# Two plain gate and up steps at the head of each half step of a decoder block, with the residual reloaded by another queue

## The chip, the core and the metric

The kernel runs on one core of one Trainium2 chip. A core has TensorE (matrix products into PSUM, here called PE), VectorE (DVE), ScalarE (ACT), GpSimd (POOL) and SyncE (SP, which here only issues transfers). Each works through its own list of instructions in order, and waits on semaphores where it needs another's result. The metric is the device time of one execution in microseconds.

## The reference: what is computed

```python
x = x + 0.5 * swiglu(rms_norm(x, ffn1_norm), w_gate1, w_up1, w_down1)     # first half step
h = rms_norm(x, mix_norm); z = h @ w_in                                   # mixing: gMLP and attention
x = x + m(z) @ w_out
x = x + 0.5 * swiglu(rms_norm(x, ffn2_norm), w_gate2, w_up2, w_down2)     # second half step

def swiglu(h, w_gate, w_up, w_down):
    return (jax.nn.silu(h @ w_gate) * (h @ w_up)) @ w_down
```

There are 512 tokens, a width of 1024 and 2816 hidden columns in each half step; everything is float32.

## The kernel before

Activations lie with the features on the partitions: eight tiles `x` of 128 features by 512 tokens. Every product is made of three matmuls of rounded parts (`w_hi`·`x_hi`, `w_hi`·`x_lo`, `w_lo`·`x_hi`); a helper, `split` (lines 139 and 140), makes the parts of a weight tile: a cast on ACT to `hi`, a subtraction on DVE to `lo`. The norm's gain is applied when `xg_hi` and `xg_lo` are made (`normed_input`, lines 180 and 181); the norm's scale `r_bc` is multiplied in behind the products. `norm_scale` makes it: two matmuls with ones sum the squares (`sq_hi` and `sq_lo`, lines 194 and 195), ACT takes the root, DVE makes one Newton step (lines 158 to 160).

**A half step** is the function `ffn`. It goes through 22 blocks of 128 hidden columns, two at a time; such a pair is a `q` ("quad"), so there are eleven. After quads 0 to 3 a **down group** adds their part of the result (line 377 loads the down weights, eight output tiles `j`, 24 matmuls of 512 columns each), after quads 4 to 7 another, after 8 to 10 a last one (18 matmuls for each `j`). In the last group line 387 adds the part, line 389 multiplies by `r_bc`, and `finish` adds the residual: it reloads `x` into a `scratch` tile by a transfer that POOL issues (line 482; line 949 in the second half step), and line 483 (950) adds it. In the first half step `finish1` then makes `xg` and the squares of the next norm, and writes `y` to `x1_dram` through POOL; in the second, SP writes the output.

A quad in its ordinary form, `quad`, takes seven half-size products in place of eight (four blocks of gate and up, combined by sums of weights, line 307, and sums of activations): 168 matmuls of 256 columns, line 320. The first product takes `xg` as it is (A11), the second takes the sums `s_hi`, `s_lo` of `half_sums`. `add_sums` makes those once for a half step, on DVE, for four pairs of tiles `kt` and `kt + 4`: two products with the gain (line 218), four sums (lines 221 to 224) and a `split`. The first half step starts with a **plain** quad instead, `first_quad`: 96 matmuls of 512 columns (lines 125 to 127), in an order that needs only `xg`, with weights in quarters of a tile while `x` still comes in; `add_sums` follows it. The second half step starts with `add_sums` and an ordinary quad 0.

Weights pass through `w_raw` tiles (two shared, four of the half step's own pool) and `w_hi`, `w_lo` tiles (three shared, one own). The own tiles of the second half step lie where the mixing's tiles lay, and can be written only after its last matmul. A scheduler lays the instructions of each engine in a fixed order at build time; a transfer that waits holds up the SP queue behind it.

Between the half steps, `pump` runs the mixing's weight units. The first four are `w_qk`, 24 matmuls each (lines 529 to 531), in the order: two units, the norm's two matmuls of `norm_scale`, a third unit, four transposes of `r_bc` (line 899), the fourth. At its end, eight units of `add_out` (line 869) make the tiles `x` of the second half step one after the other.

## Time and profile before

| | us |
|---|---|
| median of 3 runs (1195.34 to 1196.57) | 1195.42 |
| the profiled execution | 1197.43 |
| its span, from the first to the last instruction | 1195.6 |
| PE busy | 1156.7 (97%) |
| DVE busy | 868.6 (73%) |
| ACT busy | 600.5 (50%) |

Times below are microseconds from the start of the span. In the table of stretches a row holds the stretch, its length, the busy time and (in brackets) the instructions of PE, of PE's weight loads, of DVE, ACT and POOL, then the granted clock of PE (1.00 is 2.4 GHz, 0.50 is 1.2 GHz), the DMA engines' busy share and their GB/s. In a row of the timeline the numbers are start and duration; "[4.90 <-ACT sq_hi L139]" says that the engine stood idle 4.90 us before it and what ended that; "x5" that five such rows are merged. Durations of neighbours overlap a little, so a pace is read from start to start. A matmul's duration is its latency, longer than its pace.

### The profile page before, as it was taken

The page shows a single profiled execution, that of the slowest core. Times are in us where ns is not written, and L with a number is a line of the kernel's source. Part 1 is how long each engine was busy: PE and PEld are TensorE (multiplying, and loading weights), DVE is VectorE, ACT ScalarE, POOL GpSimd, SP SyncE. Part 2 cuts the span into 40 slices and gives each one's busy share as a digit, 9 for nine tenths or more (in the row PEclk, how much of TensorE's full clock was granted, in tenths as well). Part 3 has the DMA queues.
Part 4 walks back from the last instruction along what each step waited for, and adds up shares of the span by engine and source line. Part 5 has one row for each costly group of instructions (what it writes and reads, how often), then busy time and mean ns, then how long its engine had stood idle before and what let it go on. Part 6 is the DMA issues. An engine that isn't in the chain of part 4 may idle for free.

```text
span 1195.6 us, 17191 instructions
## 1 busy us (share of the span) xinstructions
PE 1156.7 (97%) x6834; PEld 1017.2 (85%) x6834; DVE 868.6 (73%) x1342; ACT 600.5 (50%) x869; POOL 37.1 (3%) x74
## 2 busy tenths in 40 slices
PE   9699999999998999999999999999699999999998
PEld 7699899989986888888888778887699889988996
DVE  7996379747877667876778876555998459855875
ACT  7454256414544454557687966333475335532540
POOL 0000000000002000000000001000000000000000
PEclk9799999999999999999999999999799999999999
DMA  7134133422335332231212124333325322441332
GB/s 247 49 101 151 56 109 107 144 68 86 120 104 164 118 89 89 60 99 59 76 62 66 46 83 145 102 115 126 112 75 159 121 66 78 136 128 53 107 124 88
DMA packets 47983, 122.11 MB, mean 102 GB/s; under 512 B 4512, under 2 KB 6592, under 8 KB 47904
## 3 DMA queue, kind: packets, MB, share of 16 engines
q1 hardware_dynamic: 44160, 109.07, 28.8%
q0 software_dynamic: 3744, 11.96, 3.1%
q8 instruction: 53, 0.87, 0.3%
q14 instruction: 26, 0.21, 0.1%
HBM read 114.72 MB, written 6.29 MB: 101 GB/s over the span
## 4 chain that ended last, share of the span: by engine, by line
PE 89%; DVE 4%; ACT 3%; DMA 2%; issue 1%; POOL 0%; POOLq 0%; DVEq 0%; ACTq 0%
PE bank_acc L320 22%; PE bank_att L320 12%; PE bank_acc L125 10%; PE bank_acc L126 9%; PE bank_acc L127 9%; PE bank_acc L530 4%; PE bank_acc L531 4%; PE bank_acc L529 4%; PE bank_att L126 4%; PE bank_att L127 4%; PE bank_att L125 4%; DMA scratch<-in_x 1%; PE bank_att L658 1%; PE bank_att L659 1%; PE bank_att L684 1%
## 5 line engine op out<-in xcount | busy, mean ns | idle before, releaser
L139 ACT CAST w_hi<-w_raw 128x1024 fp32r<-128x1024 f32 (+2 forms) x195 | 189.5, 979 | 273.7 <-PE bank_acc L126 93.2
L140 DVE TENSOR_TENSOR w_lo<-w_raw,w_hi 128x1024 fp32r<-128x1024 f32 (+2 forms) x195 | 220.0, 1133 | 69.5 <-ACT w_hi L139 68.2
L139 ACT CAST w_hi<-w_sum 128x1024 fp32r<-128x1024 f32 x84 | 88.2, 1050 | 146.6 <-PE bank_acc L320 63.1
L320 PE MATMUL bank_acc<-s_hi,w_hi 128*128 128x256 f32 x504 | 142.4, 283 | 0.9 <-ACT w_hi L139 0.9
L320 PE MATMUL bank_acc<-s_lo,w_hi 128*128 128x256 f32 x504 | 142.0, 282 | 0.0
L320 PE MATMUL bank_acc<-s_hi,w_lo 128*128 128x256 f32 x504 | 141.8, 281 | 0.0
L140 DVE TENSOR_TENSOR w_lo<-w_sum,w_hi 128x1024 fp32r<-128x1024 f32 x84 | 102.3, 1219 | 28.5 <-ACT w_hi L139 28.5
L320 PEld LDWEIGHTS bank_acc<-s_hi,w_hi 128*128 128x128 f32 x504 | 95.6, 190 | 1.6 <-ACT w_hi L139 1.5
L320 PEld LDWEIGHTS bank_acc<-s_lo,w_hi 128*128 128x128 f32 x504 | 95.4, 189 | 0.0
L320 PEld LDWEIGHTS bank_acc<-s_hi,w_lo 128*128 128x128 f32 x504 | 95.4, 189 | 0.0
L529 PE MATMUL bank_acc<-w_hi,xg_hi 128*128 128x512 f32 x224 | 90.5, 404 | 0.0
L530 PE MATMUL bank_acc<-w_lo,xg_hi 128*128 128x512 f32 x224 | 89.6, 400 | 0.0
L531 PE MATMUL bank_acc<-w_hi,xg_lo 128*128 128x512 f32 x224 | 89.3, 399 | 0.0
L320 PE MATMUL bank_acc<-xg_lo,w_hi 128*128 128x256 f32 x256 | 72.1, 282 | 0.0
L320 PE MATMUL bank_acc<-xg_hi,w_hi 128*128 128x256 f32 x256 | 72.0, 281 | 0.0
L320 PE MATMUL bank_acc<-xg_hi,w_lo 128*128 128x256 f32 x256 | 72.0, 281 | 0.0
L125 PE MATMUL bank_acc<-xg_hi,w_hi 128*128 128x512 f32 x176 | 70.8, 402 | 1.1 <-ACT w_hi L139 1.1
L320 PE MATMUL bank_att<-s_hi,w_hi 128*128 128x256 f32 x168 | 49.7, 296 | 21.7 <-ACT w_hi L139 21.7
L127 PE MATMUL bank_acc<-xg_hi,w_lo 128*128 128x512 f32 x176 | 70.4, 400 | 0.0
L126 PE MATMUL bank_acc<-xg_lo,w_hi 128*128 128x512 f32 x176 | 70.3, 399 | 0.0
L320 PE MATMUL bank_att<-xg_lo,w_hi 128*128 128x256 f32 x248 | 69.8, 282 | 0.0
L320 PE MATMUL bank_att<-xg_hi,w_hi 128*128 128x256 f32 x248 | 69.7, 281 | 0.0
(271 smaller groups left out, 2944.9 us busy)
## 6 DMA issues: line engine op xcount, KB each, us to landing
w_raw<-in_gu SPq DMA_DIRECT2D x84, 512.0 KB, 3.8
w_raw<-in_dn SPq DMA_DIRECT2D x32, 512.0 KB, 3.6
w_raw<-in_w_qk SPq DMA_DIRECT2D x16, 512.0 KB, 3.7
w_raw<-in_dn SPq DMA_DIRECT2D x16, 384.0 KB, 3.2
w_raw<-in_w_v SPq DMA_DIRECT2D x8, 512.0 KB, 3.6
w_raw<-in_w_ga SPq DMA_DIRECT2D x8, 512.0 KB, 3.5
w_raw<-in_w_gb SPq DMA_DIRECT2D x8, 512.0 KB, 3.6
w_raw<-in_w_pb SPq DMA_DIRECT2D x8, 512.0 KB, 3.6
```

Of the source, the lines that this page charges most:

```text
L125: nc.tensor.matmul(ps, lhsT=lhi, rhs=rhi, start=first, stop=False)
L126: nc.tensor.matmul(ps, lhsT=lhi, rhs=rlo, start=False, stop=False)
L127: nc.tensor.matmul(ps, lhsT=llo, rhs=rhi, start=False, stop=last)
L139: latest["hi"] = nc.scalar.copy(hi, src)
L140: latest["lo"] = nc.vector.tensor_tensor(lo, src, hi, op=ALU.subtract)
L320: nc.tensor.matmul(o, lhsT=l[:, s], rhs=r, start=first and f == kt == i == 0, stop=kt == HK - 1 and i == 2, skip_group_check=True,)
L529: nc.tensor.matmul(banks[t], lhsT=xg_hi[k][:, ts], rhs=hi[:, s], start=k == 0, stop=False)
L530: nc.tensor.matmul(banks[t], lhsT=xg_hi[k][:, ts], rhs=lo[:, s], start=False, stop=False)
L531: nc.tensor.matmul(banks[t], lhsT=xg_lo[k][:, ts], rhs=hi[:, s], start=False, stop=k == KD - 1)
L658: nc.tensor.matmul(s[m], lhsT=qd[m][:, qs], rhs=kd[m][:, :w], start=True, stop=False)
L659: nc.tensor.matmul(s[m], lhsT=ql[m][:, qs], rhs=kd[m][:, :w], start=False, stop=False)
L684: nc.tensor.transpose(ps[:, j * P : (j + 1) * P], a[:, j * P : (j + 1) * P], ident)
```

## The change

Quads 0 and 1 of both half steps are plain (`plain_quad`), and `add_sums` comes after quad 1. `add_sums` no longer multiplies whole tiles by the gain: ACT makes one scaled half tile, and four DVE instructions take `x` directly, with the gain or its negative (`neg_gains`, new) as a factor; the sums lie in tiles that the results of quads 2 and 3 take later. The second column block of the first quad loads and splits each weight tile whole, no longer in quarters. The residual is reloaded as four `x_again` tiles, through SP, in the program ahead of the last down group, into the tiles of the weight sums (`w_sum`) and of `g`; the addition stands in `ffn`. `add_out` runs in the order 0, 4, 1, 5, 2, 6, 3, 7.

```diff
         def add(kt, x1, x2):
-            y = []
-            for j, xt in ((kt, x1), (kt + HK, x2)):
-                y.append(scratch())
-                g = gains[:, norm * KD + j : norm * KD + j + 1]
-                nc.vector.tensor_scalar(y[-1], xt, g, None, op0=ALU.mult)
-            f = pool.tile([P, 4, HT], F32, name="sums", tag="g", bufs=2)
-            (a11, a21), (a12, a22) = ((t[:, :HT], t[:, HT:]) for t in y)
-            nc.vector.tensor_tensor(f[:, 1], a11, a21, op=ALU.subtract)
-            nc.vector.tensor_tensor(f[:, 0], a22, a21, op=ALU.subtract)
...
+            (x11, x21), (x12, x22) = ((t[:, :HT], t[:, HT:]) for t in (x1, x2))
+            f = pool.tile([P, 4, HT], F32, name="sums", tag=("a_hi", "a_lo")[kt % 2] + str(2 + kt // 2))
+            a21 = scratch()[:, :HT]
+            nc.scalar.activation(a21, x21, AF.Copy, scale=g1)
+            add = partial(nc.vector.scalar_tensor_tensor, op0=ALU.mult, op1=ALU.subtract)
+            add(f[:, 1], x11, g1, a21)
+            add(f[:, 0], x22, g2, a21)
+            add(f[:, 2], x22, neg, f[:, 1])
+            add(f[:, 3], x12, neg, f[:, 2])
...
-        def first_quad():
+        def plain_quad(q):
...
+                loading = load is not None and q == f == 0
+                cuts = 4 if loading else 1
...
-                    if k % 2 == 0:
-                        cs = slice(k * P, (k + 2) * P)
+                    if k % (KD // cuts) == 0:
+                        cs = slice(k * P, k * P + D // cuts)
                         for e in range(2):
-                            nc.sync.dma_start(out=raws[e][:, cs], in_=gu[f, e, :, cs])
+                            nc.sync.dma_start(out=raws[e][:, cs], in_=gu[2 * q + f, e, :, cs])
                             split(w[e][0][:, cs], w[e][1][:, cs], raws[e][:, cs])
...
-                if q == 0 and load is not None:
-                    first_quad()
+                if q < 2:
+                    plain_quad(q)
+                else:
+                    quad(q)
+                if q == 1:
                     for kt in range(HK):
                         add_sums(kt, xt[kt], xt[kt + HK])
-                    continue
-                if q == 0:
-                    for kt in range(HK):
-                        add_sums(kt, xt[kt], xt[kt + HK])
-                quad(q)
+            if f0 + n == NF:
+                for i in range(HK):
+                    tag = ("w_sum", "g")[i // 2]
+                    back.append(pool.tile([P, 2, T], F32, name="x_again", tag=tag, bufs=2))
+                    again(back[i], i)
...
                     nc.vector.tensor_tensor(y[j], y[j], r_bc, op=ALU.mult)
+                    nc.vector.scalar_tensor_tensor(
+                        y[j], y[j], -0.5, back[j // 2][:, j % 2], op0=ALU.mult, op1=ALU.add
+                    )
                     finish(j, y[j])
...
         def finish1(j, y):
-            xr = scratch()
-            nc.gpsimd.dma_start(out=xr, in_=x[:, j, :])
-            nc.vector.scalar_tensor_tensor(y, y, -0.5, xr, op0=ALU.mult, op1=ALU.add)
...
+        def again1(t, i):
+            nc.sync.dma_start(out=t, in_=x[:, 2 * i : 2 * i + 2, :])
...
-        for n in range(KD):
+        for n in (n for kt in range(HK) for n in (kt, kt + HK)):
             add_out(n)
```

**VectorE in the first plain quad**, while it sums the squares of `x` (`sq_sum`) and splits the weights of the second column block. Before:

```order
L189 TENSOR_TENSOR sq_sum_119<-sq_sum_119,scratch_277 128x512
L140 TENSOR_TENSOR w_lo_301<-w_raw_304,w_hi_300 128x256
L189 TENSOR_TENSOR sq_sum_119<-sq_sum_119,scratch_280 128x512
L140 TENSOR_TENSOR w_lo_303<-w_raw_305,w_hi_302 128x256
L189 TENSOR_TENSOR sq_sum_119<-sq_sum_119,scratch_283 128x512
L140 TENSOR_TENSOR w_lo_301<-w_raw_304,w_hi_300 128x256
L140 TENSOR_TENSOR w_lo_303<-w_raw_305,w_hi_302 128x256
```

Now:

```order
L190 TENSOR_TENSOR sq_sum_120<-sq_sum_120,scratch_279 128x512
L190 TENSOR_TENSOR sq_sum_120<-sq_sum_120,scratch_282 128x512
L140 TENSOR_TENSOR w_lo_303<-w_raw_306,w_hi_302 128x1024
L190 TENSOR_TENSOR sq_sum_120<-sq_sum_120,scratch_285 128x512
L140 TENSOR_TENSOR w_lo_305<-w_raw_307,w_hi_304 128x1024
L140 TENSOR_TENSOR w_lo_376<-w_raw_379,w_hi_375 128x1024
L140 TENSOR_TENSOR sq_lo_290<-sq_sum_120,sq_hi_289 128x512
```

The first split of that block stands one sum later and covers a whole tile, and the splits of quad 1 (`w_lo_376` is the first) follow at once.

**The SP queue around the last down group of the first half step** (`in_gu1`: gate and up weights, `in_dn1`: down weights, `in_w_qk`: the mixing's). Before:

```order
L303 DMA w_raw_3117<-in_gu1 128x2x512
L377 DMA w_raw_3350<-in_dn1 128x768
L377 DMA w_raw_3384<-in_dn1 128x768
L377 DMA w_raw_3420<-in_dn1 128x768
L377 DMA w_raw_3456<-in_dn1 128x768
L377 DMA w_raw_3492<-in_dn1 128x768
L377 DMA w_raw_3528<-in_dn1 128x768
L377 DMA w_raw_3564<-in_dn1 128x768
L377 DMA w_raw_3600<-in_dn1 128x768
L116 DMA w_raw_3640<-in_w_qk 128x1024
```

Now, from the third down load on:

```order
L384 DMA w_raw_3302<-in_dn1 128x768
L497 DMA x_again_3225<-in_x 128x1024
L384 DMA w_raw_3336<-in_dn1 128x768
L497 DMA x_again_3227<-in_x 128x1024
L384 DMA w_raw_3370<-in_dn1 128x768
L384 DMA w_raw_3404<-in_dn1 128x768
L497 DMA x_again_3229<-in_x 128x1024
L384 DMA w_raw_3438<-in_dn1 128x768
L384 DMA w_raw_3472<-in_dn1 128x768
L497 DMA x_again_3231<-in_x 128x1024
L116 DMA w_raw_3510<-in_w_qk 128x1024
```

The four reloads stand behind the third, fourth, sixth and eighth down load.

**VectorE behind the last `add_out`**, at the head of the second half step. Before:

```order
L869 TENSOR_TENSOR x1_7_7238<-x1_7_7238,bank_acc_7800 128x512
L218 TENSOR_SCALAR scratch_7837<-x1_0_7224,gains_79 128x512
L181 SCALAR_TENSOR_TENSOR xg_lo7_116<-x1_7_7238,gains_79,xg_hi7_108 128x512
L189 TENSOR_TENSOR sq_sum_119<-sq_sum_119,scratch_7828 128x512
L218 TENSOR_SCALAR scratch_7839<-x1_4_7232,gains_79 128x512
L221 TENSOR_TENSOR sums_7841<-scratch_7837 128x256
```

Now:

```order
L880 TENSOR_TENSOR x1_7_7108<-x1_7_7108,bank_acc_7670 128x512
L182 SCALAR_TENSOR_TENSOR xg_lo7_117<-x1_7_7108,gains_79,xg_hi7_109 128x512
L190 TENSOR_TENSOR sq_sum_120<-sq_sum_120,scratch_7698 128x512
L140 TENSOR_TENSOR sq_lo_7772<-sq_sum_120,sq_hi_7771 128x512
L140 TENSOR_TENSOR w_lo_7785<-w_raw_7788,w_hi_7784 128x1024
L140 TENSOR_TENSOR w_lo_7787<-w_raw_7789,w_hi_7786 128x1024
```

The squares and the weights of quad 0's second column block (`w_raw_7788`, `w_raw_7789`) come first, and the sums only after the norm.

## Rows read from the trace of the kernel before

**Rows 1.** The page: engine totals, and PE's clock in 40 slices.

```profile
PE 1156.7 (97%) x6834; PEld 1017.2 (85%) x6834; DVE 868.6 (73%) x1342; ACT 600.5 (50%) x869; POOL 37.1 (3%) x74
...
PEclk9799999999999999999999999999799999999999
```

**Rows 2.** Waits of PE over the span: total, times, longest.

```profile
PE bank_att L320 <- ACT w_hi L139: 21.7, 2, 12.0
```

**Rows 3.** Stretches: heads, ordinary quads, a down group, the seam to the mixing.

```profile
31.07:65.54 34.47, 23.59 (x169) 22.80 (x168) 32.16 (x43) 16.66 (x18) 0.00 (x0) 0.80 0.20 62
65.54:105.46 39.92, 39.92 (x338) 39.92 (x337) 35.46 (x36) 22.05 (x25) 0.00 (x0) 1.00 0.42 133
105.46:149.97 44.51, 44.51 (x194) 36.06 (x193) 17.39 (x16) 13.14 (x17) 0.00 (x0) 1.00 0.26 75
378.69:393.08 14.39, 9.49 (x31) 7.15 (x31) 7.09 (x9) 5.55 (x8) 6.31 (x11) 0.76 0.45 143
831.83:928.43 96.60, 83.36 (x675) 82.49 (x674) 89.72 (x106) 53.43 (x60) 0.54 (x1) 0.91 0.39 123
```

**Rows 4.** PE's timeline at the first head, and its first matmuls.

```profile
8.34 0.63 PE L127 MATMUL bank_att<-xg_hi,w_lo 128*128 128x512 f32 x1
8.77 0.63 PE L125 MATMUL bank_acc<-xg_hi,w_hi 128*128 128x512 f32 x1
...
43.73 0.58 PE L320 MATMUL bank_att<-s_hi,w_hi 128*128 128x256 f32 x1 [9.67 <-ACT w_hi L139]
```

**Rows 5.** VectorE's work from 26 to 47 us, by group (count, busy us, mean ns).

```profile
L140 DVE TENSOR_TENSOR s_lo<-sums,s_hi 128x1024 fp32r<-128x1024 f32 x4 | 4.9, 1220 | 0.0
L218 DVE TENSOR_SCALAR scratch<-x,gains 128x512 f32<-128x512 f32 x8 | 3.8, 478 | 0.0
...
L223 DVE SCALAR_TENSOR_TENSOR sums<-sums,scratch 128x256 f32<-128x256 f32 x4 | 1.7, 414 | 0.0
```

**Rows 6.** DVE's timeline in the first plain quad.

```profile
15.10 3.87 DVE L189 TENSOR_TENSOR sq_sum<-sq_sum,scratch 128x512 f32<-128x512 f32 x5
18.89 0.42 DVE L140 TENSOR_TENSOR w_lo<-w_raw,w_hi 128x256 fp32r<-128x256 f32 x1
```

**Rows 7.** Stretches again: 10 to 20 us, in the first plain quad.

```profile
10.00:20.00 10.00, 10.00 (x43) 8.05 (x42) 9.26 (x18) 9.98 (x23) 0.00 (x0) 1.00 0.96 330
```

**Rows 8.** Seam to the mixing: the reload (a line's view), waits, timelines of POOL, DVE and PE.

```profile
DMA to landing us min/median/max: 2.9/3.8/4.5
...
DVE y L483 <- DMA scratch<-in_x: 8.8, 6, 2.3
...
376.29 0.54 POOL L482 DMA_DIRECT2D scratch<-in_x  x1
...
367.49 0.40 PE L529 MATMUL bank_acc<-w_hi,xg_hi 128*128 128x512 f32 x1
383.75 0.79 PE L194 MATMUL bank_att<-sq_hi,ones_r 128*128 128x512 f32 x1 [4.90 <-ACT sq_hi L139]
...
379.95 0.69 DVE L483 SCALAR_TENSOR_TENSOR y<-y,scratch 128x512 f32<-128x512 f32 x1 [2.33 <-DMA scratch<-in_x]
380.56 1.22 DVE L140 TENSOR_TENSOR w_lo<-w_raw,w_hi 128x1024 fp32r<-128x1024 f32 x1
```

**Rows 9.** Last down group of the first half step: SP, DVE (timelines).

```profile
303.87 26.59 SPq L377 DMA_DIRECT2D w_raw<-in_dn  x8
...
318.22 1.22 DVE L140 TENSOR_TENSOR w_lo<-w_sum,w_hi 128x1024 fp32r<-128x1024 f32 x1
...
338.24 1.23 DVE L140 TENSOR_TENSOR a_lo<-g,a_hi 128x1024 fp32r<-128x1024 f32 x1 [1.17 <-ACT a_hi L139]
```

**Rows 10.** Second head: PE and DVE timelines, and a stretch.

```profile
846.86 0.58 PE L320 MATMUL bank_att<-s_hi,w_hi 128*128 128x256 f32 x1 [12.03 <-ACT w_hi L139]
...
826.43 0.69 DVE L869 TENSOR_TENSOR x<-x,bank_acc 128x512 f32<-128x512 f32 x1 [2.22 <-PE bank_acc L127]
...
835.00:840.00 5.00, 0.00 (x0) 0.00 (x0) 5.00 (x13) 1.05 (x1) 0.00 (x0) 0.68 1.00 376
```

More of the change, by code (lines that the diff above doesn't have):

```diff
@@ L145, in decoder_block @@
     eps_col = const.tile([P, 1], F32, name="eps_col")
+    neg_gains = const.tile([P, 3 * KD], F32, name="neg_gains")
     nc.gpsimd.dma_start(out=gains, in_=cols)
@@ L213, in add @@
         def add(kt, x1, x2):
-            y = []
-            for j, xt in ((kt, x1), (kt + HK, x2)):
-                y.append(scratch())
-                g = gains[:, norm * KD + j : norm * KD + j + 1]
-                nc.vector.tensor_scalar(y[-1], xt, g, None, op0=ALU.mult)
-            f = pool.tile([P, 4, HT], F32, name="sums", tag="g", bufs=2)
-            (a11, a21), (a12, a22) = ((t[:, :HT], t[:, HT:]) for t in y)
-            nc.vector.tensor_tensor(f[:, 1], a11, a21, op=ALU.subtract)
-            nc.vector.tensor_tensor(f[:, 0], a22, a21, op=ALU.subtract)
-            nc.vector.scalar_tensor_tensor(f[:, 2], f[:, 0], -1.0, a11, op0=ALU.mult, op1=ALU.subtract)
-            nc.vector.scalar_tensor_tensor(f[:, 3], a12, -1.0, f[:, 2], op0=ALU.mult, op1=ALU.subtract)
+            g1, g2, neg = (
+                t[:, norm * KD + j : norm * KD + j + 1]
+                for t, j in ((gains, kt), (gains, kt + HK), (neg_gains, kt + HK))
+            )
[8 more added lines that the diff above has]
+            add(f[:, 3], x12, neg, f[:, 2])
             s_hi.append(pool.tile([P, 4, HT], F32R, name=f"s_hi{kt}"))
@@ L240, in half_sums, with ffn @@
         return add, operand
-    def ffn(pool, gu, dn, norm, xt, finish, load, prepare):
+    def ffn(pool, gu, dn, norm, xt, finish, load, prepare, again):
         a_hi, a_lo = {}, {}
@@ L260, in activated @@
         def activated(q):
-            hi = pool.tile([P, 2, T], F32R, name=f"a_hi{q % 4}")
-            lo = pool.tile([P, 2, T], F32R, name=f"a_lo{q % 4}")
+            hi, lo = (pool.tile([P, 2, T], F32R, name=f"a_{n}{q}", tag=f"a_{n}{q % 4}") for n in ("hi", "lo"))
             a_hi[q], a_lo[q] = hi, lo
@@ L290, in first_quad @@
                 banks.append(ps)
-                if f == 0:
+                if q == f == 0:
                     prepare[0]()
@@ L297, in first_quad @@
                 nc.vector.scalar_tensor_tensor(g[:, f], up, -1.0, g[:, f], op0=ALU.mult, op1=ALU.mult)
-            split(*activated(0), g)
+            split(*activated(q), g)
         def quad(q):
@@ L358, in quad @@
             split(*activated(q), g)
-        y = []
+        y, back = [], []
         for f0 in range(0, NF, 8):
@@ L389, in ffn @@
                     nc.vector.tensor_tensor(y[j], y[j], r_bc, op=ALU.mult)
+                    nc.vector.scalar_tensor_tensor(
+                        y[j], y[j], -0.5, back[j // 2][:, j % 2], op0=ALU.mult, op1=ALU.add
+                    )
                     finish(j, y[j])
@@ L471, in prepare1 @@
         def prepare1():
+            nc.vector.tensor_scalar(neg_gains, gains[:, : 3 * KD], -1.0, None, op0=ALU.mult)
             for j in range(KD):
@@ L947, in finish2, with again2 @@
         def finish2(j, y):
-            xr = scratch()
-            nc.gpsimd.dma_start(out=xr, in_=x2_dram[j])
-            nc.vector.scalar_tensor_tensor(y, y, -0.5, xr, op0=ALU.mult, op1=ALU.add)
             nc.sync.dma_start(out=out[:, j, :], in_=y)
-        ffn(ff2, gu2, dn2, 2, x1, finish2, None, {0: norm_scale})
+        def again2(t, i):
+            for e in range(2):
+                nc.sync.dma_start(out=t[:, e], in_=x2_dram[2 * i + e])
+        ffn(ff2, gu2, dn2, 2, x1, finish2, None, {0: norm_scale}, again2)
 def _layouts(i):
```

4 lines of the change are left out of this document (2 added, 2 removed).

## The prediction

> **What bounds the kernel now.** The page comes first: PE is busy for 97% of the span and no other engine above 73% [rows 1]. So only two things can change the time: what PE has to do, and the few stretches in which it stands still or runs at the lower clock. The clock's row shows where to look: outside the first slice there is a dip near the start and one in the slice that holds 837 to 867 us [rows 1]. The waits of PE give three holes their sizes: 21.7 us in two waits for a cast of weights ahead of the second product of the first ordinary quad, the longest 12.0 [rows 2], and 4.9 us for the cast of the summed squares [rows 8]. Then I read the table of stretches [rows 3] and the timelines of the three places.
>
> *First head* (31.07 to 65.54, quad 1). PE does the first product, stands 9.67 us [rows 4], and goes on at a granted clock that is 0.80 over the stretch [rows 3]. The wait names a cast on ACT, but ACT is busy for 16.66 of 34.47 us and DVE for 32.16: DVE makes the activation sums, and the cast's input, a sum of weights, stands behind them on DVE. The sums cost 3.8 us of gain products, four groups of half-size sums of about 1.7 each, and 4.9 of splits, 15.4 us in all [rows 5].
>
> *Seam to the mixing.* PE reaches the norm's two matmuls at 378.69 and waits until 383.75, because the squares of the last tile are late [rows 8]. They are late because DVE waited 8.8 us in six waits for the reloaded residual; the reloads go out one by one through POOL, the last at 376.29, each 3.8 us to landing [rows 8]. Behind the hole the clock is low, 0.76 over the stretch [rows 3].
>
> *Second head* (831.83 to 928.43, quads 0 to 3). The same as the first, with a hole of 12.03 us [rows 10] and a clock of 0.91 over the stretch [rows 3].
>
> **The change part by part.** The prices of the two kinds of quad: two ordinary ones take 39.92 us, 19.96 each; a down group of 192 matmuls of 512 columns takes 44.51 us, 0.232 each, so a plain quad of 96 takes 22.3 us [rows 3]. A plain quad is thus 2.3 us dearer on PE, and three more of them 6.9 us. That is what is paid. What is got is that PE needs no activation sums for 22.3 us (first head) and 44.6 us (second).
>
> *First head.* Quad 1 took 34.47 us [rows 3]; plain, 22.3. That is 12.2 us less, if it starts without a wait and quad 2 finds its sums. The sums lose the gain products (3.8 us of DVE) and one of the four sums' inputs is now a half-tile copy on ACT, 4 of them; no such row is in the trace. Sums of 256 columns with a factor already cost the 414 ns of the others [rows 5], so 16 of them take 6.6 us, with the splits 11.5. By the order DVE has besides, between the norm and quad 2: the norm's three steps, eight evacuations of the plain quads at 0.69 at most [as the addition in rows 8], six splits of 1.22, two weight sums of the same size: about 2.1 + 5.5 + 9.8 = 17.4. Together 29 us. PE reaches the second product of quad 2 near 57.1 (31.07 + 0.9 for a wait explained below + 22.3, and 2.85 for the first product, a seventh of 19.96); the norm's steps begin near 26, where rows 5 begin, so DVE has 31 us. Two of the evacuations, one split and one weight sum (3.8 us) are not needed by then, but DVE also waits: PE gives it the last evacuation that it needs, and ACT the cast of the last weight sum, only some 4 us before the end. Some 2 us are left. I take no wait, and keep the lack of that margin for a rival.
>
> One thing is lost. The second column block of quad 0 now has its weights split whole. DVE's first split of it stood behind five sums of squares, at 18.89 [rows 6]; now it stands behind six (0.76 each by the row of five), so at 19.65, and takes 1.22 in place of 0.42 [rows 6, 8]: done at 20.8. PE begins the block at 31.07 − 50 × 0.232 = 19.5 and needs the low part at its third matmul, at 19.9. That makes a wait of 0.9 us; the bounds are 0 and 1.2 (if the sum in between also slips). The head gives 12.2 − 0.9 = 11.3 us.
>
> Does the transfer itself make this worse? In that stretch the DMA engines are busy for 0.96 and move 330 GB/s [rows 7], and ACT, which makes the first cast, is busy for 9.98 of the 10 us: the cast waits for ACT, not for its bytes. The Trainium skill (Perfetto Trace Analysis, DMA Optimizations) says that splitting transfers into smaller chunks may let some start sooner, which speaks against this merging. If the landing decided, 512 KB in place of 128 KB at the row's 330 GB/s would cost 1.2 us rather than 0.9, and the sum would be 0.3 us worse.
>
> *Second head.* Quads 2 and 3 stay as they are, so 96.60 − 39.92 = 56.7 us now go to quads 0 and 1 and the norm's two matmuls; plain they take 2 × 22.3 + 0.46 = 45.1. That is 11.6 us less, if the weights are there. The first block's weights use shared tiles; the last of those is free when the matmuls of the seventh `add_out` end, near 826.4 (the addition that waits for them starts at 826.43 [rows 10]), and a cast and a split (1.05 [rows 10] and 1.22 [rows 8]) fit before 831.8. The second block's weights need the mixing's memory and can be loaded only from 831.8 on. The row from 835 to 840 shows the queue doing just that at 376 GB/s [rows 10]: four tiles of 512 KB have landed by 840. The two needed first land before that, and two casts and splits end by about 842 at the latest; PE wants them at 831.83 + 48 × 0.232 = 843.0. The sums then have 22 us more room than at the first head. The new order of `add_out` only changes which tile comes last; the plain quad reaches its eighth tile after 10 us, so it costs nothing.
>
> *Seam to the mixing.* The reload is now issued during the last ordinary quad. What it could hold up is the SP queue. The first two `x_again` wait for the weight sums' tiles, the last of which is done with at 319.4; the third for a `g` long free; the fourth for the `g` of the last quad, done at 339.5 [rows 9]. Before them in the queue stand the third to the eighth down load. The queue issued its eight loads up to 330.5 [rows 9], and behind the fourth reload stand only weights of the mixing, which PE needs at 367.49 [rows 8]. So no down load waits for the late tile, and I cost it at nothing; if that cover failed, down loads from the fifth on would go out at 339.5, land some 4 us later, and still be early for PE, which needs the fifth at 334 + 4 × 4.2 = 350.7.
>
> With the residual there, DVE has after PE's last down matmul (367.49) two weight splits, and for the last two tiles the additions, gains, low parts and squares: 2 × 1.22 + 8 × 0.69 = 8.0 us, and about 1.2 us for links through ACT. The squares' low part is ready near 376.7, and PE gets there at 378.69: no hole, 2 us to spare. The stretch of 14.39 us then holds 26 matmuls of 0.232 and the transposes (0.35): 6.4 us. Next late are those transposes: they want `r_bc`, which I put 0.2 us after PE is there. The seam gives 14.39 − 6.4 − 0.2 = 7.8 us.
>
> *The end.* The last additions stay three DVE steps behind the last matmul, then the output: nothing.
>
> **Sum.** 11.3 + 7.8 + 11.6 = 30.7 us off the profiled execution (1197.43, its span 1195.6), 1166.7. The median of the runs is 2.0 lower, so 1195.42 − 30.7 = 1164.7.
>
> **The rivals.** *The sums are late again* (chance 0.10). For: DVE is 93% busy at the first head, and my margin there is 2 us of some 29. Against: the second head has 22 us more. Price: a wait of 2 to 5 us ahead of quad 2, and as much again at the lower clock, 4 to 8 us: 1169 to 1173.
>
> *The reload gains nothing* (0.05). The Trainium skill (DMA: Bandwidth & Descriptors, Issuing engines are not separate DMA queues) says that all issuers share the same 16 DMA engines, so another issuer saves only issue time. As a mechanism here: the residual lands as late as before, the 7.8 us stay, 1172.5. Against it: a reload took 3.8 us, the waits came from issuing it only when a `scratch` tile was free [rows 8], and the new tiles are free at 319.4. The trace bears the rule on speed, not its result.
>
> *The second head's weights are late* (0.06). If the loads behind the mixing's memory came one whole tile later (some 1.4 us each at 376 GB/s, two tiles), PE would stand about 2 us and run as long at the lower clock: 1168.
>
> *Slower than before: the plain quads run at the lower clock* (0.03). At the start of the kernel matmuls of 512 columns, behind an idle engine, ran at 1.2 GHz, 0.43 us each [rows 4]. At 0.43 the three added quads, 288 matmuls, would cost 57 us more: 1222. It decides against the change once 155 matmuls run so. Against it: PE works without a break up to both heads, at 1.00 [rows 3, 7].
>
> *The change doesn't do what it says* is bounded by the same prices: a plain quad that waits for its weights is the third rival.
>
> **How the numbers follow.** Forecast 0.74, with 1162.5 (no wait of 0.9, a little from the seam) to 1167.5; the rivals as given; 0.02 for others. The range reaches to the first two rivals: 1162.5 to 1172.5. All but the slower rival are far below 1193; this kernel's measurement can tell 0.2%, 2.4 us, from no change. So: faster 0.95, same 0.02, slower 0.03.
>
> **What would show it.** Right: in the new trace no wait of PE above 1 us between quad 0 and quad 2 of either half step, each plain quad 22.3 us, the norm's matmuls right behind the second `w_qk` unit, the clock's row without dips after the first slice. Wrong: a wait ahead of the second product of quad 2, a wait for `sq_hi`, or a DVE wait for `x_again`.

## The result, and the profile after

The changed kernel takes 1168.55 us (median of four executions: 1167.13, 1167.15, 1169.95, 1170.63) against 1195.95 for the kernel before beside it: a ratio of 0.9772, 95% interval 0.9752 to 0.9792. A second set of four gave 1167.62 (1167.22 to 1168.92; ratio 0.9760, 0.9747 to 0.9773); the median of all eight is 1167.6, and the experiments below are read against that. The forecast was 1164.7, with a range of 1162.5 to 1172.5. The way and the range were right; of the gain, 27.4 to 28.5 us came in place of 30.7.

The page of the changed kernel, engine totals and PE's clock in 40 slices, answers to [rows 1]:

```profile
PE 1153.1 (99%) x6618; PEld 1002.2 (86%) x6618; DVE 836.8 (72%) x1294; ACT 589.6 (51%) x856; POOL 29.7 (3%) x58
...
PEclk9999999999999999999999999999999999999999
```

The dips in the clock's row are gone, and PE has 216 matmuls fewer: three quads of 168 gave way to three of 96. Its waits over the span (total, times, longest) answer to [rows 2]:

```profile
PE bank_acc L125 <- ACT w_hi L139: 2.1, 2, 1.4
PE bank_acc L127 <- DVE w_lo L140: 1.2, 1, 1.2
PE bank_att L156 <- DVE eps_col L151: 1.1, 1, 1.1
```

The waits of 21.7 and 4.9 us are gone. The first two rows are one place, the second column block of the first quad, all but 0.7 us ahead of the first matmul; the third stood before the change too. The stretches that answer to [rows 3] (columns as there) are quads 2 and 3 of the first half step, its last down group with the seam up to the next stretch of plain matmuls, the first two quads of the second half step, and its first four:

```profile
54.64:94.46 39.82, 39.82 (x337) 39.82 (x336) 33.89 (x34) 22.40 (x26) 0.00 (x0) 1.00 0.42 133
...
322.85:379.91 57.06, 57.06 (x248) 45.57 (x247) 43.23 (x61) 28.69 (x39) 11.22 (x18) 1.00 0.41 131
...
813.12:858.16 45.04, 45.04 (x195) 36.43 (x194) 33.90 (x46) 22.68 (x28) 0.54 (x1) 1.00 0.38 123
...
813.12:897.99 84.87, 84.87 (x532) 76.25 (x530) 67.85 (x79) 44.76 (x53) 0.54 (x1) 1.00 0.40 128
```

PE is busy for the whole of each, at full clock. The same seam in the kernel before took 64.89 us, of which PE was busy for 59.99:

```profile
333.87:398.76 64.89, 59.99 (x249) 47.44 (x247) 43.30 (x61) 28.86 (x39) 13.30 (x24) 0.95 0.42 134
```

So the profiled spans part like this. Up to the first down group: 105.46 before, 94.46 after, 11.0 us. Seam: 64.89 − 57.06 = 7.8. Second head up to its down group: 96.6 − 84.87 = 11.7. The rest of the span is 0.3 us longer. Together 30.2, which is 1195.6 − 1165.4.

The one hole left is in the first quad. PE's timeline of the changed kernel, its first matmul, the end of the first column block, the two waits and the start of quad 2:

```profile
5.60 0.51 PE L125 MATMUL bank_acc<-xg_hi,w_hi 128*128 128x512 f32 x1 [0.69 <-ACT w_hi L139]
...
17.38 0.40 PE L127 MATMUL bank_att<-xg_hi,w_lo 128*128 128x512 f32 x1
19.22 0.49 PE L125 MATMUL bank_acc<-xg_hi,w_hi 128*128 128x512 f32 x1 [1.44 <-ACT w_hi L139]
19.55 0.40 PE L126 MATMUL bank_acc<-xg_lo,w_hi 128*128 128x512 f32 x1
21.14 0.50 PE L127 MATMUL bank_acc<-xg_hi,w_lo 128*128 128x512 f32 x1 [1.19 <-DVE w_lo L140]
...
54.64 0.28 PE L324 MATMUL bank_acc<-xg_hi,w_hi 128*128 128x256 f32 x1
```

And what it waits for, on ACT and then on DVE:

```profile
13.88 0.71 ACT L181 ACTIVATE xg_hi<-x,gains 128x512 fp32r<-128x512 f32 x1
14.49 3.75 ACT L189 ACTIVATE scratch<-x 128x512 f32<-128x512 f32 x7
18.14 3.88 ACT L139 CAST w_hi<-w_raw 128x1024 fp32r<-128x1024 f32 x4
...
15.28 4.67 DVE L190 TENSOR_TENSOR sq_sum<-sq_sum,scratch 128x512 f32<-128x512 f32 x6
19.87 1.22 DVE L140 TENSOR_TENSOR w_lo<-w_raw,w_hi 128x1024 fp32r<-128x1024 f32 x1
```

The seven squares of `x` stand on ACT right behind the last `xg_hi`, and the four casts (two of this block, two of quad 1) behind them. The first cast ends near 19.2, and there PE's first wait ends. DVE's split stands behind six sums of these squares and ends at 21.1, where the second wait ends.

### The profile page after: what moved, and what is told of

Same layout as the page of the kernel before. It is cut to its first block, busy times and chain, and to the rows that moved or that the text cites. A ratio compares the mean times of both kernels' runs of the same rounds, so it can differ in the third digit from the quotient of the medians.

```text
span 1165.4 us, 16669 instructions
## 1 busy us (share of the span) xinstructions
PE 1153.1 (99%) x6618; PEld 1002.2 (86%) x6618; DVE 836.8 (72%) x1294; ACT 589.6 (51%) x856; POOL 29.7 (3%) x58
## 4 chain that ended last, share of the span: by engine, by line
PE 94%; ACT 2%; DVE 2%; DMA 1%; issue 0%; SPq 0%; DVEq 0%; ACTq 0%
PE bank_acc L324 20%; PE bank_att L324 11%; PE bank_acc L127 11%; PE bank_acc L125 11%; PE bank_acc L126 11%; PE bank_att L127 5%; PE bank_att L126 5%; PE bank_att L125 5%; PE bank_acc L542 4%; PE bank_acc L541 4%; PE bank_acc L540 4%; PE bank_att L669 1%; DMA x<-in_x 1%; PE bank_att L670 1%; PE bank_att L695 1%
## 5 line engine op out<-in xcount | busy, mean ns | idle before, releaser
L324 PE MATMUL bank_acc<-s_lo,w_hi 128*128 128x256 f32 x432 | 121.6, 281 | 0.0
L324 PE MATMUL bank_acc<-s_hi,w_hi 128*128 128x256 f32 x432 | 121.5, 281 | 0.0
L324 PE MATMUL bank_acc<-s_hi,w_lo 128*128 128x256 f32 x432 | 121.4, 281 | 0.0
L126 PE MATMUL bank_acc<-xg_lo,w_hi 128*128 128x512 f32 x224 | 88.9, 397 | 0.1
L125 PE MATMUL bank_att<-a_hi,w_hi 128*128 128x512 f32 x176 | 69.4, 394 | 0.0
L125 PE MATMUL bank_acc<-a_hi,w_hi 128*128 128x512 f32 x176 | 69.4, 394 | 0.0
L126 PE MATMUL bank_att<-a_lo,w_hi 128*128 128x512 f32 x176 | 69.4, 394 | 0.0
L126 PE MATMUL bank_acc<-a_lo,w_hi 128*128 128x512 f32 x176 | 69.4, 394 | 0.0
L127 PE MATMUL bank_acc<-a_hi,w_lo 128*128 128x512 f32 x176 | 69.4, 394 | 0.0
L127 PE MATMUL bank_att<-a_hi,w_lo 128*128 128x512 f32 x176 | 69.4, 394 | 0.0
```

The lines of the kernel that those rows point to most:

```text
L125: nc.tensor.matmul(ps, lhsT=lhi, rhs=rhi, start=first, stop=False)
L126: nc.tensor.matmul(ps, lhsT=lhi, rhs=rlo, start=False, stop=False)
L127: nc.tensor.matmul(ps, lhsT=llo, rhs=rhi, start=False, stop=last)
L324: nc.tensor.matmul(o, lhsT=l[:, s], rhs=r, start=first and f == kt == i == 0, stop=kt == HK - 1 and i == 2, skip_group_check=True,)
```

## Experiments

The label in brackets behind each heading is the run's name in the tables and texts below.

**The changed kernel itself, again (again_as_is).** No edit.

> The changed kernel itself, run again. Its four executions so far fall into two pairs, 1167.1 and 1170.0 to 1170.6, with mean granted clocks of 0.999 and 0.997. Theory A: the pairs differ in what PE's clock does after PE stands still at 17.6 to 21.1 us (waits of 1.44 and 1.19 us ahead of the second column block of the first quad). Then the executions again lie near 1167 or near 1170, and a profile of one of the long ones has the lower clock within some 25 us of that hole. Rival B: they differ in the first 11 us, where the profile of the kernel before had matmuls of 0.43 us each and that of the changed kernel 0.232. That can't make a long execution, since PE then only comes later to a block whose weights come no sooner: the pairs would differ by under 0.5 us.

Measured: 1167.22, 1167.60, 1168.92, 1167.64, with clocks of 0.999, 0.999, 0.998, 0.999. There are no two clean pairs, and its profile is again a short execution (span 1165.4), so this run alone settles nothing. The long executions came into view in the profiles of the runs below. Seven profiles have the same first head, up to the start of quad 2:

| profile | span | last `xg_hi` on ACT | second block's first matmul | quad 2's first matmul | clock behind the hole |
|---|---|---|---|---|---|
| the changed kernel | 1165.4 | 13.88 | 19.22 | 54.64 | 1.00 |
| again_as_is | 1165.4 | 14.02 | 19.36 | 54.78 | 1.00 |
| add_out_in_turn | 1165.6 | 14.14 | 19.48 | 54.91 | 1.00 |
| one_plain_second | 1172.7 | 14.17 | 19.52 | 54.94 | 1.00 |
| reload_by_pool | 1167.1 | 15.30 | 20.66 | 56.09 | 1.00 |
| gain_products_kept | 1167.1 | 14.02 | 19.36 | 56.33 | 0.59 |
| reload_by_scratch | 1173.5 | 15.29 | 20.64 | 57.60 | 0.52 |

Two things add up: quad 2 starts 40.8 us behind the last `xg_hi` in every profile whose clock stayed at 1.00, and 42.3 us behind it in the two where it fell. In the profile of reload_by_pool the last tile of `x` came later, and the last `xg_hi` starts at 15.30 in place of 13.88; ACT's squares, the casts and the second block follow 1.4 us later. (The tile's transfer left the SP queue at 10.03, in the changed kernel at 8.94, so 1.1 us of this arose before the transfer.)

```profile
15.30 0.72 ACT L181 ACTIVATE xg_hi<-x,gains 128x512 fp32r<-128x512 f32 x1 [0.69 <-DMA x<-in_x]
...
20.66 0.50 PE L125 MATMUL bank_acc<-xg_hi,w_hi 128*128 128x512 f32 x1 [1.25 <-ACT w_hi L139]
```

In those of gain_products_kept and reload_by_scratch the clock fell right behind the two waits. The stretch of gain_products_kept that begins with the matmul that ended the second wait:

```profile
21.29:25.50 4.21, 4.21 (x12) 3.34 (x13) 4.21 (x5) 1.38 (x2) 0.00 (x0) 0.59 0.55 162
```

The same of reload_by_scratch:

```profile
22.56:26.10 3.54, 3.54 (x9) 2.78 (x10) 3.54 (x5) 1.39 (x2) 0.00 (x0) 0.52 0.62 167
```

Twelve matmuls in 4.21 us are 0.35 each in place of 0.232, so this costs some 1.4 us in that stretch. Late `x` alone gives +1.5 at quad 2, the clock alone +1.7 (0.14 of it a later `xg_hi`), both +3.0; the changed kernel's own long executions have spans of 1168.2 and 1168.9, 2.8 and 3.5 above the short ones, with a clock of 0.997. That fits both at once, but none of these was traced. Theory A holds in part (the lower clock does stand behind the hole, but the pairs are not its work alone). Rival B falls: the executions differ by up to 3.5 us, and in the profile of add_out_in_turn, a short execution, PE's first matmuls did run at the lower clock, with quad 2 no later for it.

**The second block in quarters, as before (cuts_kept).**

```diff
-                cuts = 4 if loading else 1
+                cuts = 4 if load is not None and q == 0 else 1
```

> The changed kernel with one edit taken back: the second column block of the first quad is loaded and split in quarters of a tile, as before the change. Theory A (the hole at 17.6 us is there because whole tiles pass through ACT and DVE): the first quarter is cast 0.38 after 18.1 and its low part follows by 19.3, so PE waits some 1.3 us less, and the clock has less of a hole to fall behind: the lower pair at 1165.8, the higher pair gone or rarer. Theory B (what counts is when ACT is done with the squares, near 18.1, and not the size of the pieces): the wait shrinks by under 0.7 us, 1166.5 or more, and both pairs stay. By the forecast on record, 0.9 us.

Measured: 1166.29 (1166.14 to 1166.53), 1.3 us under the changed kernel (1.0 between the shortest executions of the two), all five executions within 0.4. PE waits for the low parts for 0.23 and 0.22 us, and quad 2 starts at 53.95, 39.7 us behind the last `xg_hi` (14.27) in place of 40.8:

```profile
18.53 2.54 ACT L139 CAST w_hi<-w_raw 128x256 fp32r<-128x256 f32 x8
...
19.94 0.50 PE L127 MATMUL bank_acc<-xg_hi,w_lo 128*128 128x512 f32 x1 [0.23 <-DVE w_lo L140]
21.82 0.50 PE L127 MATMUL bank_acc<-xg_hi,w_lo 128*128 128x512 f32 x1 [0.22 <-DVE w_lo L140]
```

The casts still start only behind the squares, at 18.53, but the first now takes a quarter. (Here PE's first matmuls ran at the lower clock, as in [rows 4], so it also came later to the block, and the profile doesn't show how long it would have waited for the first cast.) The median lies between the two theories, 0.5 us above theory A's time and 0.2 us under theory B's; the long executions are gone, as theory A said. The price of the whole tiles is 1.1 us in the profiles and 1.3 by the medians, not 0.9.

**The squares behind the second block's weights (squares_later).**

```diff
-                if q == f == 0:
+                if q == 0 and f == (load is not None):
                     prepare[0]()
```

> The changed kernel with the squares of the first norm placed in the program behind the second column block's loads and splits, not ahead of them; tiles stay whole. Theory B (ACT's seven squares, 3.75 us from 14.49, hold up the cast of the weights): the casts start near 14.6 and both waits, 2.63 us in all, go: 1164.5, and with the hole the higher pair at 1170. Theory A: as theory B if the tiles have landed by 15. Rival, by the landing of whole tiles: if 512 KB land only near 18, the wait stays at 1.5 us or more and the time at 1166 or above. What is late next: the norm's scale, some 2 us later, which delays the sums; if they were on the edge, a wait of 1 to 3 us ahead of the second product of quad 2.

Measured: 1165.34 (1165.27 to 1166.19; ratio to the kernel before 0.9741, 0.9727 to 0.9754), 2.3 us under the changed kernel, and every execution under each of its eight. Both waits in quad 0 are gone with whole tiles:

```profile
16.00 1.05 ACT L139 CAST w_hi<-w_raw 128x1024 fp32r<-128x1024 f32 x1 [1.05 <-DMA w_raw<-in_gu]
17.28 1.05 ACT L139 CAST w_hi<-w_raw 128x1024 fp32r<-128x1024 f32 x1 [0.23 <-DMA w_raw<-in_gu]
...
58.82 0.39 PE L324 MATMUL bank_acc<-s_hi,w_lo 128*128 128x256 f32 x1 [0.67 <-DVE w_lo L140]
```

ACT now waits for the landing of the tiles, until 16.0, and still casts in time. So the squares ahead of the casts are the cause, as theory B says; the size of the pieces counts only behind them, where quarters took 1.1 to 1.3 us off (cuts_kept). The edit moves the squares on ACT and their sums on DVE together, so the share of each is not separated. What the expectation named as late next did come: DVE is behind by 0.67 us inside quad 2, quads 2 and 3 take 40.75 us in place of 39.82, and the time stays 0.8 us above the 1164.5 expected. This is the lowest median measured; squares_between and sums_early below have ratios of 0.9743 and 0.9745 to the kernel before, which the intervals don't tell from its 0.9741.

**One plain quad at the second head (one_plain_second).**

```diff
+        plain = 2 if load is not None else 1
...
-                if q < 2:
+                if q < plain:
...
-                if q == 1:
+                if q == plain - 1:
```

> The changed kernel with one plain quad, not two, at the head of the second half step (sums behind it, quad 1 ordinary). If the sums are ready by the second product of quad 1, 25 us behind the head, the second plain quad is worth nothing and costs 22.3 less 19.96: this one is 2.3 us faster, 1166.2. If VectorE is as full there as at the first head (a hole of 9.67 us in the kernel before, behind one plain quad, with 3.8 us of gain products that are gone now), PE waits 3 to 8 us and runs as long at the lower clock: 1171 to 1180.

Measured: 1174.25 (1173.67 to 1174.37), 6.6 us over the changed kernel, the rival's case. PE's timeline with the waits in its quad 1, and then the stretch from the head to the down group:

```profile
841.64 0.38 PE L324 MATMUL bank_att<-s_hi,w_hi 128*128 128x256 f32 x1 [1.39 <-ACT s_hi L139]
843.09 0.57 PE L324 MATMUL bank_att<-s_lo,w_hi 128*128 128x256 f32 x1 [1.07 <-DVE s_lo L140]
844.62 0.58 PE L324 MATMUL bank_acc<-s_hi,w_lo 128*128 128x256 f32 x1 [0.74 <-DVE w_lo L140]
848.42 0.58 PE L324 MATMUL bank_att<-s_lo,w_hi 128*128 128x256 f32 x1 [1.51 <-DVE s_lo L140]
```

```profile
813.27:905.28 92.01, 87.28 (x604) 81.73 (x603) 77.63 (x88) 49.32 (x58) 0.54 (x1) 0.94 0.37 118
```

4.7 us of holes and a mean clock of 0.94: 92.01 − 84.87 = 7.1 us more in the profile, though 2.3 us of plain quad are saved.

**The squares between the loads and the matmuls of the second block (squares_between).**

```diff
+                early = load is not None and q == 0 and f == 1
+                if early:
+                    for c in range(0, D, D // 1):
+                        for e in range(2):
+                            cs = slice(c, c + D // 1)
+                            nc.sync.dma_start(out=raws[e][:, cs], in_=gu[f, e, :, cs])
+                            split(w[e][0][:, cs], w[e][1][:, cs], raws[e][:, cs])
+                    prepare[0]()
                 for k in range(KD):
...
-                    if k % (KD // cuts) == 0:
+                    if not early and k % (KD // cuts) == 0:
...
-                if q == f == 0:
+                if q == f == 0 and load is None:
                     prepare[0]()
```

> The changed kernel with both splits of the first quad's second column block (whole tiles) placed ahead of the squares, and the squares and the norm's matmuls ahead of that block's matmuls, not behind them as in squares_later. squares_later lost 0.9 us of its gain again at quad 2 (0.67 us of wait for a low part), where VectorE came later because the norm's matmuls stood behind the whole block on PE and the root came 5 us later (norm's first step at 33.2, in the changed kernel 28.1). Theory: here the norm's matmuls stand inside the block, the first step comes by 30, quads 2 and 3 take 40.0 us again, and the time is that of squares_later less 0.9: 1164.4. Rival: the squares on ACT end only near 20.5, and PE then waits for them at the norm's matmuls inside the block: 1166 or more.

Measured: 1165.77 (1165.68 to 1165.84), not 1164.4. Quads 2 and 3 are back at 39.8 us (53.43 to 93.25), as expected, but a wait of 0.94 us came earlier:

```profile
25.58 0.50 PE L127 MATMUL bank_acc<-xg_hi,w_lo 128*128 128x512 f32 x1 [0.94 <-DVE w_lo L140]
```

That is quad 1's first weight tile, whose split stands behind six sums of squares on DVE. The rival named another place, so both missed; moving the squares moved the wait to another tile, and did not remove it.

**The residual of the first half step through POOL into scratch tiles, as before (reload_by_scratch).**

```diff
         def finish1(j, y):
+            xr = scratch()
+            nc.gpsimd.dma_start(out=xr, in_=x[:, j, :])
+            nc.vector.scalar_tensor_tensor(y, y, -0.5, xr, op0=ALU.mult, op1=ALU.add)
             normed_input(j, y, 1)
...
-        ffn(ff1, gu1, dn1, 0, xt, finish1, load1, {0: prepare1, 5: constants1}, again1)
+        ffn(ff1, gu1, dn1, 0, xt, finish1, load1, {0: prepare1, 5: constants1}, None)
```

> The changed kernel with the reload of the first half step taken back (one tile at a time into scratch tiles through POOL, from finish1); the second half step keeps its x_again. Theory: the wait ahead of the norm's column sums (4.90 us) and the lower clock behind it come back, 7.8 us on the 1167.6 of the kernel run again: 1175.4. Rival by the page's rule on shared DMA engines (the reload itself gains nothing, the gap closed for another reason): 1167.6.

Measured: 1173.80 (1173.09 to 1175.25), 6.2 us over the changed kernel, where 7.8 were expected. The seam has its hole again (PE's timeline, then the stretch):

```profile
375.15 0.51 PE L195 MATMUL bank_att<-sq_hi,ones_r 128*128 128x512 f32 x1 [2.52 <-ACT sq_hi L139]
```

```profile
325.81:387.73 61.92, 57.80 (x248) 45.35 (x247) 44.20 (x61) 28.77 (x39) 13.32 (x24) 1.00 0.43 141
```

With its neighbours the hole makes 61.92 − 57.06 = 4.9 us in this profile, with no lower clock behind it. The rival falls: the reload carries the seam. The wait is 2.5 us here and 4.90 in [rows 8] because, counted from the first matmul of the last down group, PE came to the norm's matmuls 1.8 us later (1.09 of it a wait in the `w_qk` units) and the squares were ready 0.5 us sooner.

**The same tiles, loaded through POOL (reload_by_pool).**

```diff
-            nc.sync.dma_start(out=t, in_=x[:, 2 * i : 2 * i + 2, :])
+            nc.gpsimd.dma_start(out=t, in_=x[:, 2 * i : 2 * i + 2, :])
```

> The changed kernel with the four x_again transfers of the first half step issued by POOL and not by SP, at the same place of the program, into the same tiles. Theory (what counts is that tiles are free by 320 to 340 us, 30 us before the residual is needed): nothing changes, 1167.6 within 0.6. Rival (the queue counts): VectorE waits for x_again and the seam loses up to 7.8 us: 1169 to 1175.

Measured: 1168.08 (1166.98 to 1170.96): no change. POOL issued the four as their tiles came free, the last at 330.20, 26 to 28 us before they are needed (the first tile at 334.13, the last pair from 357.98):

```profile
307.83 0.54 POOL L497 DMA_DIRECT2D x_again<-in_x  x1 [142.28 <-DVE w_lo L140]
310.17 0.53 POOL L497 DMA_DIRECT2D x_again<-in_x  x1 [1.80 <-DVE w_lo L140]
311.44 0.53 POOL L497 DMA_DIRECT2D x_again<-in_x  x1 [0.73 <-DVE a_lo L140]
330.20 0.53 POOL L497 DMA_DIRECT2D x_again<-in_x  x1 [18.23 <-DVE a_lo L140]
```

What counts is that the tiles are free early, not which queue fills them. The Trainium skill (DMA: Bandwidth & Descriptors, Issuing engines are not separate DMA queues) says that all issuers share the same DMA engines; this run agrees, 1168.08 against 1167.6.

**One plain quad at the first head (one_plain_first).** The edit is that of one_plain_second, with `1 if load is not None else 2`.

> The changed kernel with one plain quad at the head of the first half step (sums in their new form behind it), two in the second. Theory (a second plain quad is what covers the sums): the sums' new form takes some 2.5 us of VectorE off (8 products of 0.48 go, 16 sums grow from 0.41 to 0.48), so the hole of 9.67 us shrinks to about 7 and the clock falls behind it as before: 11.0 less 2.5 to 4 us dearer than the changed kernel, 1174.6 to 1176.1. Rival (the new form of the sums carries the gain at the first head, the plain quad little): under 1170.

Measured: 1177.07 (1175.91 to 1179.53), 9.5 us over the changed kernel and above the expectation's 1174.6 to 1176.1. Its longest wait of PE:

```profile
PE bank_att L324 <- DVE w_lo L140: 6.0, 1, 6.0
```

The hole shrank from 9.67 to 6.0 us, as expected, but this profile also has late `x` and the lower clock behind the first quad's hole. The second plain quad, more than the new form of the sums, carries the first head.

**The reload alone, in the kernel before (reload_alone).** `x_again`, its four transfers through SP and the addition in `ffn`, as in the change; all else as before.

> The kernel before with one part of the change alone: the residual of the first half step reloaded as x_again by SP, as in the changed kernel. The forecast on record has 7.8 us for this part, of which 4.9 are the wait for the squares and the rest the lower clock behind it: 1196.1 less 7.8, 1188.3. Taking the part back out of the changed kernel cost 6.2 us (1173.8), with a wait of only 2.5 us there and the clock at 1.00 in its profile. Theory: the part is worth 5 to 8 us, by whether the clock falls behind the hole in an execution: 1188 to 1191. Rival (its worth came only with the plain quads, which shift the phase of the clock): under 4 us, 1192 or more.

Measured: 1189.91 (1189.02 to 1190.59) against 1196.98, ratio 0.9945 (0.9932 to 0.9958): 7.1 us by the medians, 6.6 by the ratio. Its seam is that of the changed kernel:

```profile
333.50:390.53 57.03, 57.03 (x248) 45.59 (x247) 43.87 (x61) 28.66 (x39) 10.10 (x18) 1.00 0.40 132
```

57.03 against 57.06, so in the profile the part gives 64.89 − 57.03 = 7.9 us without any plain quad.

**The sums in their old form (gain_products_kept).**

```diff
-            a21 = scratch()[:, :HT]
-            nc.scalar.activation(a21, x21, AF.Copy, scale=g1)
...
+            for xt, gn in ((x1, g1), (x2, g2)):
+                y.append(scratch())
+                nc.vector.tensor_scalar(y[-1], xt, gn, None, op0=ALU.mult)
```

> The changed kernel with the sums made as before the change (two whole-tile products with the gain on VectorE, then four sums), in the new place and the new tiles. Theory: in the changed kernel the last low part of the sums is done at 49.0 us and quad 2 needs it at 57.5, so some 2.5 us more of VectorE fit: 1167.6 within 0.6, and the new form of the sums is worth nothing behind two plain quads. Rival (the margin was the 2 us of the forecast): a wait of 1 to 3 us ahead of the second product of quad 2, 1169 to 1172.

Measured: 1168.45 (1167.64 to 1168.78), within the changed kernel's spread; there is no wait ahead of quad 2's second product. DVE's last low part of the sums in the changed kernel, with the product that reads them on PE:

```profile
47.78 1.23 DVE L140 TENSOR_TENSOR s_lo<-sums,s_hi 128x1024 fp32r<-128x1024 f32 x1
...
57.47 0.28 PE L324 MATMUL bank_att<-s_hi,w_hi 128*128 128x256 f32 x1
```

And here:

```profile
55.16 1.22 DVE L140 TENSOR_TENSOR s_lo<-sums,s_hi 128x1024 fp32r<-128x1024 f32 x1
...
59.17 0.28 PE L326 MATMUL bank_att<-s_hi,w_hi 128*128 128x256 f32 x1
```

In the changed kernel the sums end at 49.0, 8.5 us ahead of the product; here at 56.4, 2.8 us ahead of it, in a profile whose lower clock behind the hole starts quad 2 some 1.5 us later. The new form is worth a margin, and no time.

**`add_out` in its old order (add_out_in_turn).**

```diff
-        for n in (n for kt in range(HK) for n in (kt, kt + HK)):
+        for n in range(KD):
```

> The changed kernel with add_out in the order 0 to 7, as before the change. The forecast on record costs the new order at nothing: 1167.6 within 0.6, and the second head as in the changed kernel (84.9 us from its first matmul to the down group). Rival (the order is what lets the sums start on a pair early): the sums end later than 851, but PE needs them only at 861; a wait only if they end 10 us later: 1170.

Measured: 1167.99 (1167.42 to 1168.73), no change.

**squares_later with the sums between quads 0 and 1 (sums_early).**

```diff
-                if q == 1:
+                if q == (load is None):
                     for kt in range(HK):
                         add_sums(kt, xt[kt], xt[kt + HK])
```

> squares_later with the activation sums of the first half step placed in the program between quads 0 and 1, not behind quad 1. squares_later lost 0.67 us at the second product of quad 2, where a low part of a weight sum stands behind the sums and evacuations on VectorE. Theory: the sums go into the time in which VectorE waits for the norm's root, the wait goes, 1164.5. Rival (VectorE is full from 30 to 60 us, so any order of the same work ends at the same time): 1165.3, as squares_later.

Measured: 1165.83 (1165.25 to 1166.42). The wait in quad 2 stays, at 0.6 us: the rival. This order of the same work found no room on DVE between 30 and 60 us; others were not tried.

## Why the prediction was right, and where it was off

**The three places and their mechanism: right.** The seam was forecast at 7.8 us and gave 7.8 in the profiles, 7.1 by the medians when added alone and 6.2 when taken out. The second head was forecast at 11.6 and gave 11.7; its two plain quads take 45.04 us with the norm's matmuls, where 45.1 stood. At the seam the norm's matmuls follow the second `w_qk` unit without a gap:

```profile
367.71 0.40 PE L195 MATMUL bank_att<-sq_hi,ones_r 128*128 128x512 f32 x1
367.94 0.40 PE L196 MATMUL bank_att<-sq_lo,ones_r 128*128 128x512 f32 x1
```

**The reload's place in the SP queue: right.** SP's timeline, to be read beside [rows 9]:

```profile
314.26 0.43 SPq L497 DMA_DIRECT2D x_again<-in_x  x1
316.27 3.17 SPq L384 DMA_DIRECT2D w_raw<-in_dn  x2
328.48 0.33 SPq L497 DMA_DIRECT2D x_again<-in_x  x1
337.60 4.39 SPq L116 DMA_DIRECT2D w_raw<-in_w_qk  x2
```

The fourth reload waited for the last `g` until 328.48 (339.5 in the forecast, less the 11.0 us of the first head), and behind it stood only weights of the mixing.

**The first head: its size nearly right, 11.0 for 11.3; one step of the working was wrong, and it cost nothing.** The step "PE begins the block at 31.07 − 50 × 0.232 = 19.5" failed. It took PE's arrival from the one profiled execution, in which the first eleven matmuls ran at the lower clock [rows 4]; in the changed kernel's most of these ran at 0.232 us, and PE was there at 17.6. So the hole was 2.63 us long, not 0.9, and the prediction's own sign of being right, no wait of PE above 1 us there, failed too (1.44 and 1.19). But the length of the hole is not its price: the block goes on when DVE's split is done, 21.1 for the forecast's 20.8, however early PE comes. In the profile of add_out_in_turn PE came at 19.15, 1.5 us later than in the changed kernel's, and the block's third matmul still started only at 21.41:

```profile
18.92 0.40 PE L127 MATMUL bank_att<-xg_hi,w_lo 128*128 128x512 f32 x1
19.48 0.50 PE L125 MATMUL bank_acc<-xg_hi,w_hi 128*128 128x512 f32 x1 [0.17 <-ACT w_hi L139]
...
21.41 0.50 PE L127 MATMUL bank_acc<-xg_hi,w_lo 128*128 128x512 f32 x1 [1.19 <-DVE w_lo L140]
```

That is 7.3 us behind the last `xg_hi` in both. In the kernel before, quad 1 started at 31.07 [rows 3], 17.4 us behind the last `xg_hi`:

```profile
13.69 0.71 ACT L180 ACTIVATE xg_hi<-x,gains 128x512 fp32r<-128x512 f32 x1
```

In the changed kernel it starts 18.5 us behind (at 32.3, which is 54.64 less the 22.3 of a plain quad; the last `xg_hi` at 13.88). So the whole tiles cost 1.1 us, close to the 0.9 of the forecast and for its reason, DVE's split. What it left out is the lower clock behind the hole, in some executions. And it had the row that pointed to a better cure (ACT busy for 9.98 of 10 us, [rows 7]) and said that the cast waits for ACT, but priced only DVE's split: squares_later shows 2.3 us by the medians, of which the quarters alone give back 1.3. As to the Trainium skill's rule on splitting transfers (Perfetto Trace Analysis, DMA Optimizations): splitting did help here, 1166.29 against 1167.6, but not by the landing: the casts stood behind the squares until 18.53 (cuts_kept), and with the squares out of their way whole tiles were no slower (1165.34).

**The margin of the sums: mis-sized.** The forecast left VectorE some 2 us ahead of quad 2's second product. The sums ended 8.5 us ahead of it, and the last piece that VectorE makes for it, the low part of its weights, 4.9 us ahead, at 52.56:

```profile
51.33 1.23 DVE L140 TENSOR_TENSOR w_lo<-w_sum,w_hi 128x1024 fp32r<-128x1024 f32 x1
```

From the norm's first step at 28.11 VectorE took 24.5 us to there, near the 29 − 3.8 = 25.2 of the forecast (though the 16 sums took 0.48 each, not 0.414). What did not come is the waiting for PE and ACT for which some 4 us were left. The first rival therefore had less of a chance than given, with two plain quads; with one, at either head, it is what happens (6.6 and 9.5 us).

**From the profile to the median: the step that cost the most.** The forecast for the span was 1195.6 − 30.7 = 1164.9, and the profiled span is 1165.4. But "The median of the runs is 2.0 lower" was carried over as if it were a property of the kernel. It says only that the profiled execution of the kernel before was a long one beside the other three; the medians of the four sets on record, 1195.95 to 1196.98, lie 0.5 to 1.5 us under it. Of the 2.9 us between 1164.7 and 1167.6 this step makes 2.5. Executions of both kernels spread over some 3.5 us (1194.9 to 1198.5 before), and the profiled one of the changed kernel is the shortest of its eight, 0.5 us under their median and 1.4 under that of the first four. The kernel before's own spread goes with the clock: on record its executions with a mean clock of 0.987 took 1194.9 to 1195.9, those with 0.984 and 0.985 1196.0 to 1198.5. Where in the kernel the difference lies was not traced.

**The other rivals.** The reload gains nothing: fell. The second head's weights come late: no such wait. The plain quads at the lower clock: not over whole quads, but in a small form: some ten matmuls behind the first quad's hole, in some executions, 1.5 us.

## What to carry to other kernels

Where PE waits for a derived operand behind a full VectorE, more work on PE that doesn't need the operand can be the cure: 2.3 us more for each plain quad bought back holes of 9.67 and 12.03 us with the low clock behind them, and one quad too few gave up 9.5 of 11.0 us at the first head and 6.6 of 11.7 at the second. When an edit enlarges pieces (whole tiles in place of quarters), look at what stands ahead of the first piece on every engine that it passes, and price the chain that ends last; how long PE stands there says little, since it may only have come early. And subtract a saving from the profiled execution only; how far that one lies from the median has to be known for each kernel.

## What the runs showed of the hardware that was not expected

PE's clock behind the two waits in the first quad fell in three of the eight profiles that have them (0.59 and 0.52 over the stretches above, 0.59 in that of one_plain_first) and stayed at 1.00 in five. The length of the waits did not decide it: the clock fell behind 0.71 and 1.20 us (gain_products_kept) and not behind 1.44 and 1.19 us (the changed kernel). Where it fell, quad 2 came 1.5 us later. What decides it is not shown.

With the same transfers in the same order, ACT could make the last `xg_hi` at 13.88 to 15.30 us in the seven profiles of the table, and quad 2 came later by as much, whenever PE had come: behind a chain that hangs on the last tile of `x`, this goes straight into the time. The executions of cuts_kept and squares_between lie within 0.4 and 0.2 us. Those of squares_later and sums_early, which have no hole there either, lie within 0.9 and 1.2 us, so the hole is not the whole of the spread, and four or five executions each don't say more.
